# Transformer block with delta rule and dilated attention: the gate's modulation summed along with the second group's levels, sums of C11 made where they are read, T4 and the last turns on ScalarE

## The chip, the core and the metric

The kernel runs on one core of one Trainium2 chip. It has a matrix engine (TensorE, PE in the profile), a vector engine (VectorE, DVE), a scalar engine (ScalarE, ACT), GpSimd (POOL) and an engine that here only issues transfers (SyncE, SP). Each engine executes its own instructions strictly in the order in which the program lists them, and waits where an operand isn't there yet. The metric is the device time of one execution in microseconds. Three runs of the kernel before took 1418.77, 1416.32 and 1415.34 us; the median is 1416.32.

## The reference, cut to what matters

One block of a network over 1024 rows of 1024 columns, all in 32-bit floats:

```python
mod = silu(c) @ w_ada + b_ada                       # 6 parts of 1024: sh1, sc1, g1, sh2, sc2, g2
h = rmsnorm(x, norm_attn_g) * (1 + sc1) + sh1
q_a, k_a, v_a, q_d, k_d, v_d, z_d, b_d, a_d = split(h @ w_in)
y_attn = dilated_attention(q_a, k_a, v_a, rel_bias)   # 8 heads of 64
y_delta = gated_deltanet(q_d, ..., z_d)               # 8 heads of 64, 16 chunks of 64 rows
x = x + g1 * (concat(y_attn, y_delta) @ w_out)        # g1 is the gate of the change
h = rmsnorm(x, norm_ffn_g) * (1 + sc2) + sh2
x = x + g2 * ((silu(h @ w_gate) * (h @ w_up)) @ w_down)
return rmsnorm(x, final_norm_g)
```

`g1` is a row of 1024 numbers: the product of silu(c) with 1024 columns of `w_ada`, plus `b_ada`. The kernel uses it to scale the columns of `w_out`.

## The kernel before, in words

Every large product is made of three matmuls per 128x128x512 step: each operand is split into a high part (a rounded copy, `wh`, `hh`, `T3h`) and a low part (what the rounding left, `wl`, `hl`, `T3l`), and high x high, high x low and low x high are added up in one bank of the accumulator.

The program runs in these stages; times are in the span of the profiled execution. First comes the head with the norm and the first projections. Then the delta rule for heads 0 to 3 (`delta(0)`) and heads 4 to 7 (`delta(1)`). Each group has an inversion on DVE (31 pairs of small products into `tt`), a trip of the inverse through memory that reorders it (`tn_d`, then `tn`), a **level stage** that builds the larger blocks of the inverse for four heads (`head`: `lv` by PE, `cs` by DVE, `lb` by PE, `lw` by PE, `tc` by DVE, `lx` by PE), and a scan over eight double chunks (`delta_scan`). For the second group the inversion ends at 366 us, the level stage lies between 373 and 407 us, and the scan follows to about 449 us. While those small steps run, the remaining projections (`g_a`, `g_va`) fill PE between them; a table of numbers (`FILL`, `LEVELS`, `TURNS`) says how much of it goes where.

The **attention stage** (from about 455 us) runs over 32 units (a pair of heads and a block of 128 rows): `S` scores by PE, maximum by DVE into `sc`, exponential on ACT or POOL, turns `tr`, `et`, values. Projections go on between them until the eighth unit (`free`); after that the first half of the output product `wo` fills. In the same units the rest of the modulation is summed. A slab of `w_ada` (128 rows by 512 columns, 256 KB) is loaded by SP into one of two slots (`mod_in`, tile `wm`), DVE multiplies it by 128 values of silu(c) and adds it to a running sum (`mod_add`, line 1334 for the first of eight slabs, line 1336 for the others), and after eight slabs PE sums over the 128 partitions with a matmul of ones (`mod_out`, `mods`, line 1346). Slabs 0 to 15 are the gate `g1` (two halves of 512 columns; DVE adds each sum to a broadcast of the bias in `g1r`, line 1347), slabs 16 to 47 are later parts, 48 to 63 come in the last stage. `mod_until(n)` does slabs up to n: eight at the start, then one more with each unit until unit 8, then the others spread over the rest. `out_slab` loads a slab of `w_out`, multiplies it by `g1r` on POOL and splits it.

Then the first product of the last network starts (from about 700 us, `wg`, `wu`), while the rows of x are normed and turned (`out_turn`, half of the turns by DVE and half by ACT). It uses a recursive scheme with seven products per 2x2 blocks, whose operands are `H11`, `H21`, `T1`, `T2`, `T3`, `T4`, `H22`, each split by `h2_split` (high part by ACT, low part by DVE; for T4 both by DVE). `up_first` makes `C11`: one product into bank a, copied by ACT (`p1`), another into bank b, added by DVE. `up_rest` adds to bank a the product with T2, copies the bank (`u2`, line 1664), adds the T3 product to the same bank, and later the T4 product. So the T3 matmuls cannot start before the `u2` copy by ACT has read the bank, and the T4 matmuls not before the addition by DVE (line 1620, `wg_u`) has read it again. From about 814 us to the end PE works without a gap.

Of the kernel before, what the change touches and what calls it, by code (L numbers as in the profile page):

```python
# [10 lines left out]
F32 = mybir.dt.float32  # L11
# [7 lines left out]
P = 128  # L19
# [69 lines left out]
def build(tc, I, out):  # L89
# [890 lines left out]
    def delta_scan(g, st):  # L980
# [94 lines left out]
            nc.scalar.dma_start(_.yd[g][:, :, tk].rearrange("q p t -> p q t"), yt)  # L1075

        kept, outs = {}, {}
        for n in range(8 + 3):
            if n < 8:
                state(n)  # L1080
            if 1 <= n <= 8:
                outs[n - 1] = readout(n - 1, *kept.pop(n - 1))
            if n >= 3:
                flip(n - 3, outs.pop(n - 3))
# [21 lines left out]
    def va_end(c):  # L1106
        f = va_evac(c)

        def g(tb, ps):
            f(tb, ps)  # L1110
            if c == 0:
                nc.sync.dma_start(Rb_d[tb], R_d[tb : tb + 1, :].to_broadcast([P, 1152]))
        return g

    done = set()
    def others():
# [223 lines left out]
    def mod_out(i):  # L1340
        t0 = 16 + 4 * i
        acc = states[:, HALF * (i % 2) : HALF * (i % 2) + HALF]
        ps = tbank(f"mods{i}")
        if i < 2:
            cs = slice(HALF * i, HALF * i + HALF)
            nc.tensor.matmul(ps, ones, acc, start=True, stop=True)
            nc.vector.tensor_tensor(out=g1r[:, cs], in0=ps, in1=g1r[:, cs], op=ALU.add)
            return
        v = acc.rearrange("p (t j m) -> p j t m", j=4, m=32)
        for j in range(4):  # L1350
            nc.tensor.matmul(
                ps[32 * j : 32 * j + 32, 0:P], ones[:, 0:32], v[:, j], start=True, stop=True, skip_group_check=True
            )
        t = (pa if i < 6 else po2).tile([P, 256], F32, name=f"mt{i}", tag="mt", bufs=1)
        by_columns(ps, mod[:, t0 : t0 + 4], 4, bada[:, t0 : t0 + 4], shape=t)
        if i == 5:
            nc.vector.scalar_tensor_tensor(
                out=G2, in0=mod[:, 32:40], scalar=1.0, in1=gff, op0=ALU.add, op1=ALU.mult
            )
# [7 lines left out]
    def out_slab(k, s):  # L1367

        n = slabs_made[0]
        slabs_made[0] += 1  # L1370
        p, h, b = (pe, "e", 4) if n >= 12 else (wp, "w", 5) if n % 7 < 5 else (pr, "v", 2)
        raw = wp.tile([P, slot], F32, name=f"wr_wo{k}_{s}", tag="wr", bufs=3)
        hi = p.tile([P, slot], F32R, name=f"wh_wo{k}_{s}", tag=f"{h}h", bufs=b)
        lo = p.tile([P, slot], F32R, name=f"wl_wo{k}_{s}", tag=f"{h}l", bufs=b)
        with urgent():
            nc.sync.dma_start(raw, I["wo"][k * P : (k + 1) * P, columns(s)])
            nc.gpsimd.tensor_tensor(out=raw, in0=raw, in1=g1r[:, columns(s)], op=ALU.mult)
            nc.scalar.copy(hi, raw)
            nc.gpsimd.tensor_tensor(out=lo, in0=raw, in1=hi.bitcast(F32), op=ALU.subtract)
        return hi, lo  # L1380
# [34 lines left out]
    weight = [2.0 if qb < 4 else 1.0 for _hp, qb in units]  # L1415
    xs, ets = {}, {}
    loaded[0] = att_load(0)
    nc.sync.dma_start(g1r, I["bada1"].to_broadcast([P, D]))
    summed = [0]

    def mod_until(n):
        while summed[0] < n:
# [5 lines left out]
                turns_out.append(summed[0] // 8 - 1)  # L1428

    turns_out = []  # L1430
    for n in range(2):
        mod_in(n)
    ahead(LEAD)
    mod_until(8)
    for i in range(len(units) + AV):
        while turns_out:
            mod_out(turns_out.pop(0))
        mod_until(9 + i if i < free else 16 + -(-32 * (i - free + 1) // (len(units) + AV - free)))
        if i == free:
            run(fill[0])  # L1440
            share[0] = 0.0
            sh_.close()
            spv.close()
            pr, spr = pool("pr", side="right")
            py, sy = pool("py", side="right")
            pyd, syd = pool("pyd", side="right")
            for k in range(KT):
                p_ = py if k < 4 else pyd
                yh[k] = p_.tile([P, T], F32R, name=f"yh{k}", tag=f"yh{k}")
                yl[k] = p_.tile([P, T], F32R, name=f"yl{k}", tag=f"yl{k}")  # L1450
            for k in range(4, 8):
                y_load(k, _.yd[k // 2 - 2][k % 2])
            fill[0] = out_delta()
            spent[0] = 0.0
        if i < free:
            share[0] = (W_IN - spent[0]) * weight[i] / sum(weight[i:free]) / 2
        elif free < i < len(units):
            share[0] = (W_OUT - spent[0]) * weight[i] / sum(weight[i:]) / 2
        if i < len(units):
            hp, qb = units[i]  # L1460
            if hp not in loaded:
                loaded[hp] = att_load(hp)
            if qb >= 2 and hp < 3 and hp + 1 in done and hp + 1 not in loaded:
                loaded[hp + 1] = att_load(hp + 1)
            xs[i] = [att_score(hp, qb, e) for e in range(2)]
        if AT <= i < len(units) + AT:
            hp, qb = units[i - AT]
            ets[i - AT] = [att_turn(hp, qb, e, xs[i - AT][e]) for e in range(2)]
            del xs[i - AT]
        if i >= AV:  # L1470
            hp, qb = units[i - AV]
            att_value(hp, qb, ets.pop(i - AV))
        if i == free + 12:
            for k in range(EARLY):
                y_load(k, _.ya[k])
# [28 lines left out]
    def out_turn(tb, hs):  # L1504

        hf, ts_ = tb // 4, slice(tb % 4 * P, tb % 4 * P + P)
        for q in range(2):
# [4 lines left out]
            with urgent():  # L1512
                for j in range(4):
                    d = 4 * q + j
                    if j % 2:
                        nc.vector.tensor_scalar(
                            out=x2[d, hf][:, ts_], in0=ps[:, j * P : (j + 1) * P],
                            scalar1=G2[:, d : d + 1], scalar2=mod[:, 24 + d : 25 + d], op0=ALU.mult, op1=ALU.add,
                        )
                    else:  # L1520
                        nc.scalar.activation(
                            x2[d, hf][:, ts_], ps[:, j * P : (j + 1) * P], AF.Identity,
                            bias=mod[:, 24 + d : 25 + d], scale=G2[:, d : d + 1],
                        )
# [99 lines left out]
    def up_first(f, w, raws):  # L1624
# [4 lines left out]
        with urgent():  # L1629
            nc.scalar.copy(p1, a)  # L1630
        up_mm(b, raws[1], f"{w}{f}_12", "H21")
        with urgent():
            add(p1, b, p1)
        return a, p1
# [53 lines left out]

    def up_end(f, first):
        ag, g11, rg = first["wg"] if first else gate_first(f, "wg")  # L1690
        silu(g11, g11)
        if first:
            rg = again0 if f == 0 else raws_first(f, "wg")
# [3 lines left out]
        silu(g22, g22)  # L1697
        silu(g21, bank)
        au, c11, ru = first["wu"] if first else gate_first(f, "wu")

        a11, a12, a21, a22 = (po2.tile([P, HALF], F32, name=f"a{i}_{f}", tag=f"a{i}", bufs=1) for i in (11, 12, 21, 22))
        nc.vector.tensor_tensor(out=a11, in0=g11, in1=c11, op=ALU.mult)
# [63 lines left out]
        h2_split("H22", k, x2[4 + k, 1], nc.vector)  # L1766
    for k in range(4):
        sub(x2[4 + k, 0], x2[4 + k, 0], t2[k])
        h2_split("T4", k, x2[4 + k, 0], nc.vector, nc.vector.tensor_copy)
    sx.close()  # L1770
    po2, so2 = pool("po2")

# [234 lines left out]
```

## Time and profile before

| what | us |
|---|---|
| median of three runs | 1416.32 |
| the profiled execution, device time | 1419.05 |
| its span in the trace | 1417.3 |
| PE busy | 1341.3 (95%) |
| DVE busy | 926.0 (65%) |
| ACT busy | 658.3 (46%) |
| POOL busy | 286.9 (20%) |

The mean clock that was granted to PE is 0.986 of full speed. A row of the timeline gives the start in the span, the duration, the engine, the line of the program, the operation, the tiles written and read, their shapes, and in brackets the idle time of the engine just before it with what ended it. A row of the windows gives for a stretch of time the busy time of each engine with the number of instructions, the granted clock of PE, the share of the transfer engines that was in use, and the rate in GB/s.

### The profile page before, as it was taken

What the parts mean: (1) busy time and instruction counts of PE and PEld (TensorE: products, weight loads), DVE (VectorE), ACT (ScalarE), POOL (GpSimd) and SP (SyncE); (2) the same over time, 40 slices, a digit from 0 to 9 for tenths busy, and PEclk for the clock granted to TensorE, in tenths of its full rate; (3) what the DMA queues carried; (4) which work ended last, traced back from release to release, by engine and by line L of the source; (5) the groups of instructions that cost most, each with busy time, mean ns of one, the idle gap of its engine ahead of it and who ended that gap; (6) DMA issues with size and microseconds to landing.
All of it is one profiled execution on the core that took longest, in us unless ns stands there. A gap on an engine that the chain in (4) does not pass through costs nothing.

```text
span 1417.3 us, 23510 instructions
## 1 busy us (share of the span) xinstructions
PE 1341.3 (95%) x8504; PEld 1103.1 (78%) x8504; DVE 926.0 (65%) x1761; ACT 658.3 (46%) x1302; POOL 286.9 (20%) x260
## 2 busy tenths in 40 slices
PE   7998999899998878998999799999999999999997
PEld 4776977889798766676788688888888888888886
DVE  3687875667455246767637987757575776474487
ACT  3497444383323435555659433333333333444446
POOL 2335432435214344564500000000000000000000
PEclk9999999999999989999999899999999999999999
DMA  8764343443414956667343374546363656766667
GB/s 303 232 165 133 102 154 120 137 140 90 126 32 120 246 164 199 195 187 228 127 177 111 121 223 159 175 139 195 106 217 118 194 193 195 262 214 201 196 219 244
DMA packets 161886, 243.00 MB, mean 171 GB/s; under 512 B 32647, under 2 KB 67768, under 8 KB 161769
## 3 DMA queue, kind: packets, MB, share of 16 engines
q1 hardware_dynamic: 147048, 229.96, 51.8%
q10 hardware_dynamic: 14720, 11.54, 2.4%
q8 instruction: 67, 1.10, 0.3%
q14 instruction: 51, 0.41, 0.1%
HBM read 178.68 MB, written 67.48 MB: 174 GB/s over the span
## 4 chain that ended last, share of the span: by engine, by line
PE 67%; DVE 13%; DMA 8%; ACT 4%; issue 4%; POOL 3%; SPq 0%; ACTq 0%; DVEq 0%; POOLq 0%
PE wua L1611 8%; PE wga L1611 8%; PE X L1820 7%; PE wo L1387 5%; PE wuc L1611 4%; PE Z L1820 4%; PE wgc L1611 4%; DMA wm<-in_wada 3%; PE g_a L597 3%; PE g_va L620 3%; PE Y L1820 2%; PE wub L1611 2%; PE wgb L1611 2%; PE g_vd L597 2%; PE vd L505 1%
## 5 line engine op out<-in xcount | busy, mean ns | idle before, releaser
L1601 DVE TENSOR_TENSOR wl_db<-wr_db,wh_db 128x512 fp32r<-128x512 f32 x77 | 53.2, 691 | 76.2 <-ACT wh_db L1600 75.8
L1600 ACT CAST wh_db<-wr_db 128x512 fp32r<-128x512 f32 x77 | 47.9, 622 | 98.8 <-PE X L1820 41.3
L1273 ACT ACTIVATE X<-X,sc 128x128 f32<-128x128 f32 (+7 forms) x64 | 49.7, 777 | 75.3 <-DVE sc L1268 72.5
L1275 POOL TENSOR_SCALAR X<-X,sc 128x128 f32<-128x128 f32 (+7 forms) x64 | 50.2, 786 | 98.2 <-DVE sc L1274 88.3
L1336 DVE SCALAR_TENSOR_TENSOR states<-wm,cc,states 128x512 f32<-128x512 f32 x56 | 46.9, 837 | 35.0 <-DMA wm<-in_wada 34.7
L1820 PE MATMUL X<-wl_db,wh_da 128*128 128x512 f32 x176 | 68.7, 391 | 0.5 <-DVE wl_db L1601 0.5
L1820 PE MATMUL X<-wh_db,wl_da 128*128 128x512 f32 x176 | 68.6, 390 | 0.0
L1820 PE MATMUL X<-wh_db,wh_da 128*128 128x512 f32 x176 | 68.4, 390 | 0.0
L1387 PE MATMUL wo<-wh_wo,yl 128*128 128x512 f32 x128 | 51.0, 398 | 3.7 <-DVE yl L1411 3.7
L1387 PE MATMUL wo<-wh_wo,yh 128*128 128x512 f32 x128 | 54.0, 422 | 0.5 <-ACT yh L1410 0.5
L1601 DVE TENSOR_TENSOR wl_da<-wr_da,wh_da 128x512 fp32r<-128x512 f32 x77 | 52.7, 686 | 1.2 <-ACT wh_da L1600 1.2
L597 PE MATMUL g_a<-hh,wh_a 128*128 128x512 f32 x128 | 51.9, 406 | 0.0
L1287 PE MATMUL tr<-ident,X 128*128 128x128 f32 x288 | 44.7, 283 | 7.6 <-ACT et L1292 3.1
L597 PE MATMUL g_a<-hl,wh_a 128*128 128x512 f32 x128 | 51.7, 404 | 0.0
L1268 DVE CUSTOM_DVE_ANT_0 X<-S,ng 128x512 f32<-128x512 f32 (+3 forms) x64 | 37.4, 585 | 21.2 <-PE S L1265 16.0
L1387 PE MATMUL wo<-wl_wo,yh 128*128 128x512 f32 x128 | 51.2, 400 | 0.0
L597 PE MATMUL g_a<-hh,wl_a 128*128 128x512 f32 x128 | 51.0, 399 | 0.0
L1600 ACT CAST wh_da<-wr_da 128x512 fp32r<-128x512 f32 x77 | 47.3, 616 | 5.8 <-PE wua L1611 5.8
L1600 ACT CAST wh_wg_s<-wg_s 128x512 fp32r<-128x512 f32 x33 | 20.5, 622 | 59.7 <-PE wuc L1611 22.6
L1287 PEld LDWEIGHTS tr<-ident,X 128*128 128x128 f32 x288 | 33.6, 144 | 18.0 <-POOL X L1275 5.8
L1600 ACT CAST wh_wg<-wr_wg 128x512 fp32r<-128x512 f32 x33 | 20.5, 622 | 49.9 <-PE wua L1611 18.9
L1600 ACT CAST wh_wu_s<-wu_s 128x512 fp32r<-128x512 f32 x33 | 20.4, 620 | 49.6 <-PE wga L1611 16.5
(524 smaller groups left out, 4362.7 us busy)
## 6 DMA issues: line engine op xcount, KB each, us to landing
wr_da<-ao_d SPq DMA_DIRECT2D x77, 256.0 KB, 3.2
wm<-in_wada SPq DMA_DIRECT2D x64, 256.0 KB, 3.4
wr_wg<-in_wg SPq DMA_DIRECT2D x48, 256.0 KB, 3.1
wr_wu<-in_wu SPq DMA_DIRECT2D x48, 256.0 KB, 2.7
ao_d<-a SPq DMA_DIRECT2D x44, 256.0 KB, 2.8
wr_wd<-in_wdn SPq DMA_DIRECT2D x44, 256.0 KB, 3.1
wr_db<-wt_d SPq DMA_DIRECT2D x44, 256.0 KB, 2.7
ao_d<-as SPq DMA_DIRECT2D x33, 256.0 KB, 2.8
```

Source lines behind the costliest of these rows:

```text
L597: last[0] = nc.tensor.matmul(ps, a[:, w0], b[k0 + k4][:, cs], start=(i == 0), stop=(i == n - 1))
L620: last[0] = nc.tensor.matmul(ps[:, :n], a[k][:, ts_], b[:, w0], start=(i == 0), stop=(i == 23))
L1268: nc.vector.tensor_tensor_reduce(out=X[:, c0:c1], in0=ps[:, 0 : c1 - c0], in1=ng[:, u + c0 : u + c1], scale=1.0, scalar=(3e38 if m is None ...
L1273: nc.scalar.activation(X[:, 0:nk], X[:, 0:nk], AF.Exp, scale=-1.0, bias=m, accum_out=sc[:, 2:3])
L1275: nc.gpsimd.tensor_scalar(out=X[:, 0:nk], in0=X[:, 0:nk], scalar1=sc[:, 3:4], scalar2=0.0, op0=ALU.mult, op1=ALU.add)
L1287: nc.tensor.transpose(ps[:, (kb - c0) * P : (kb - c0 + 1) * P], X[:, kb * P : kb * P + P], ident)
L1336: nc.vector.scalar_tensor_tensor(out=acc, in0=w, scalar=cc[:, k : k + 1], in1=acc, op0=ALU.mult, op1=ALU.add)
L1387: last[0] = nc.tensor.matmul(ps, a[k0 + k][:, ts_], b, start=(k == 0 and n == 0), stop=(k == 3 and n == 2))
L1600: nc.scalar.copy(hi, src)
L1601: (eng or nc.vector).tensor_tensor(out=lo, in0=src, in1=hi.bitcast(F32), op=ALU.subtract)
L1611: last[0] = nc.tensor.matmul(ps, a[:, w0], b, start=(first and k == 0 and n_ == 0), stop=(k == 3 and n_ == 2), skip_group_check=True,)
L1820: nc.tensor.matmul(bank[b], a[:, ts_], w, start=(first and f == 0 and n_ == 0), stop=(f == NF - 1 and n_ == 2), skip_group_check=True,)
```

## The change

Three things change.

First, the sixteen slabs of the gate `g1` leave the attention stage. Their loads (`gate_in`) and sums (`gate_add`) are written in `delta_scan` of the second group, two per double chunk, with slots from the tag `tm` (two, shared with the small products of the inversion). The sum runs in `g1r` itself, which POOL sets to zero early in the program and whose first row is loaded with the bias. Two matmuls of ones (`gate_out`) at the units 1 and 2 of the attention sum over the partitions, and ACT copies the result back into `g1r`. In the attention the sums then begin with slab 16 and go on at one per unit up to slab 47; the eight slabs at its start and the broadcast of the bias are gone.

Second, in the first two blocks of the last network `up_first` no longer adds the second bank into `C11` by DVE out of the accumulator: ACT copies bank b too (`p2`), and DVE adds the two copies in `up_end`, just before they are read. The high parts of T4 are rounded by ACT instead of DVE, and the last block of rows is turned by ACT alone.

Third, slab 11 of `w_out` takes its slots from another pool (`pr` instead of `wp`).

```diff
--- before.py
+++ after.py
@@ -1075,9 +1075,16 @@
             nc.scalar.dma_start(_.yd[g][:, :, tk].rearrange("q p t -> p q t"), yt)
 
         kept, outs = {}, {}
+        if g == 1:
+            for n in range(2):
+                gate_in(n)
         for n in range(8 + 3):
             if n < 8:
                 state(n)
+                if g == 1:
+                    for i in (2 * n, 2 * n + 1):
+                        gate_add(i)
+                        gate_in(i + 2)
             if 1 <= n <= 8:
                 outs[n - 1] = readout(n - 1, *kept.pop(n - 1))
             if n >= 3:
@@ -1111,6 +1118,31 @@
             if c == 0:
                 nc.sync.dma_start(Rb_d[tb], R_d[tb : tb + 1, :].to_broadcast([P, 1152]))
         return g
+
+
+    gate_w = {}
+    nc.gpsimd.memset(g1r, 0.0)
+    nc.sync.dma_start(g1r[0:1, :], I["bada1"])
+
+    def gate_in(n):
+        if n < 16:
+            i, k = n // KT, n % KT
+            gate_w[n] = pd.tile([P, HALF], F32, name=f"wm_{i}_{k}", tag="tm", bufs=2)
+            nc.sync.dma_start(gate_w[n], I["wada"][k * P : (k + 1) * P, 2 * D + HALF * i : 2 * D + HALF * i + HALF])
+
+    def gate_add(n):
+        i, k = n // KT, n % KT
+        acc = g1r[:, HALF * i : HALF * i + HALF]
+        nc.vector.scalar_tensor_tensor(
+            out=acc, in0=gate_w.pop(n), scalar=cc[:, k : k + 1], in1=acc, op0=ALU.mult, op1=ALU.add
+        )
+
+    def gate_out(i):
+
+        ps = tbank(f"gate{i}")
+        acc = g1r[:, HALF * i : HALF * i + HALF]
+        nc.tensor.matmul(ps, ones, acc, start=True, stop=True)
+        nc.scalar.copy(acc, ps)
 
     done = set()
     def others():
@@ -1341,11 +1373,6 @@
         t0 = 16 + 4 * i
         acc = states[:, HALF * (i % 2) : HALF * (i % 2) + HALF]
         ps = tbank(f"mods{i}")
-        if i < 2:
-            cs = slice(HALF * i, HALF * i + HALF)
-            nc.tensor.matmul(ps, ones, acc, start=True, stop=True)
-            nc.vector.tensor_tensor(out=g1r[:, cs], in0=ps, in1=g1r[:, cs], op=ALU.add)
-            return
         v = acc.rearrange("p (t j m) -> p j t m", j=4, m=32)
         for j in range(4):
             nc.tensor.matmul(
@@ -1368,7 +1395,7 @@
 
         n = slabs_made[0]
         slabs_made[0] += 1
-        p, h, b = (pe, "e", 4) if n >= 12 else (wp, "w", 5) if n % 7 < 5 else (pr, "v", 2)
+        p, h, b = (pe, "e", 4) if n >= 12 else (pr, "v", 2) if n in (5, 6, 11) else (wp, "w", 5)
         raw = wp.tile([P, slot], F32, name=f"wr_wo{k}_{s}", tag="wr", bufs=3)
         hi = p.tile([P, slot], F32R, name=f"wh_wo{k}_{s}", tag=f"{h}h", bufs=b)
         lo = p.tile([P, slot], F32R, name=f"wl_wo{k}_{s}", tag=f"{h}l", bufs=b)
@@ -1415,8 +1442,7 @@
     weight = [2.0 if qb < 4 else 1.0 for _hp, qb in units]
     xs, ets = {}, {}
     loaded[0] = att_load(0)
-    nc.sync.dma_start(g1r, I["bada1"].to_broadcast([P, D]))
-    summed = [0]
+    summed = [16]
 
     def mod_until(n):
         while summed[0] < n:
@@ -1428,14 +1454,15 @@
                 turns_out.append(summed[0] // 8 - 1)
 
     turns_out = []
-    for n in range(2):
+    for n in range(16, 18):
         mod_in(n)
     ahead(LEAD)
-    mod_until(8)
     for i in range(len(units) + AV):
+        if i in (1, 2):
+            gate_out(i - 1)
         while turns_out:
             mod_out(turns_out.pop(0))
-        mod_until(9 + i if i < free else 16 + -(-32 * (i - free + 1) // (len(units) + AV - free)))
+        mod_until(16 + min(i, 32))
         if i == free:
             run(fill[0])
             share[0] = 0.0
@@ -1512,7 +1539,7 @@
             with urgent():
                 for j in range(4):
                     d = 4 * q + j
-                    if j % 2:
+                    if j % 2 and tb < TB - 1:
                         nc.vector.tensor_scalar(
                             out=x2[d, hf][:, ts_], in0=ps[:, j * P : (j + 1) * P],
                             scalar1=G2[:, d : d + 1], scalar2=mod[:, 24 + d : 25 + d], op0=ALU.mult, op1=ALU.add,
@@ -1629,6 +1656,12 @@
         with urgent():
             nc.scalar.copy(p1, a)
         up_mm(b, raws[1], f"{w}{f}_12", "H21")
+        if f < AHEADF:
+
+            p2 = po.tile([P, HALF], F32, name=f"p2_{w}{f}", tag="p2", bufs=4)
+            with urgent():
+                nc.scalar.copy(p2, b)
+            return a, (p1, p2)
         with urgent():
             add(p1, b, p1)
         return a, p1
@@ -1688,6 +1721,9 @@
 
     def up_end(f, first):
         ag, g11, rg = first["wg"] if first else gate_first(f, "wg")
+        if first:
+            add(g11[0], *g11)
+            g11 = g11[0]
         silu(g11, g11)
         if first:
             rg = again0 if f == 0 else raws_first(f, "wg")
@@ -1697,6 +1733,9 @@
         silu(g22, g22)
         silu(g21, bank)
         au, c11, ru = first["wu"] if first else gate_first(f, "wu")
+        if first:
+            add(c11[0], *c11)
+            c11 = c11[0]
 
         a11, a12, a21, a22 = (po2.tile([P, HALF], F32, name=f"a{i}_{f}", tag=f"a{i}", bufs=1) for i in (11, 12, 21, 22))
         nc.vector.tensor_tensor(out=a11, in0=g11, in1=c11, op=ALU.mult)
@@ -1766,7 +1805,7 @@
         h2_split("H22", k, x2[4 + k, 1], nc.vector)
     for k in range(4):
         sub(x2[4 + k, 0], x2[4 + k, 0], t2[k])
-        h2_split("T4", k, x2[4 + k, 0], nc.vector, nc.vector.tensor_copy)
+        h2_split("T4", k, x2[4 + k, 0], nc.vector)
     sx.close()
     po2, so2 = pool("po2")
 
```

The program is ordered by a scheduler, so the instructions do not stand where the text has them. The place of the level stage, on DVE: `tt` is the last step of the inversion, `U`, `cs`, `tc` are steps of the levels, `g1r<-wm` is a sum of the gate. Before:

```order
L900 TENSOR_TENSOR tt_3816<-tt_3816,tm_30_3909 128x31
L936 STREAM_TRANSPOSE U_0_4337<-tn_3912 32x8x32 x4
L942 TENSOR_TENSOR cs_0_4339<-lv_0_4340,nbp_1350 32x256 x2
L962 TENSOR_TENSOR tc_0_4338<-lw_0_4410,nbp_1350 64x512
L942 TENSOR_TENSOR cs_1_4427<-lv_1_4428,nbp_1350 32x256
```

and in the changed kernel (three sums stand ahead of `U` in the order, of which the third is shown):

```order
L1136 SCALAR_TENSOR_TENSOR g1r<-wm_2_4779,cc,g1r 128x512
L936 STREAM_TRANSPOSE U_0_4339<-tn_3914 32x8x32 x4
L1136 SCALAR_TENSOR_TENSOR g1r<-wm_3_4782,cc,g1r 128x512
L1136 SCALAR_TENSOR_TENSOR g1r<-wm_4_4807,cc,g1r 128x512
L1136 SCALAR_TENSOR_TENSOR g1r<-wm_5_4810,cc,g1r 128x512
L1136 SCALAR_TENSOR_TENSOR g1r<-wm_6_4852,cc,g1r 128x512
L1136 SCALAR_TENSOR_TENSOR g1r<-wm_7_4855,cc,g1r 128x512
L1136 SCALAR_TENSOR_TENSOR g1r<-wm_0_4899,cc,g1r 128x512
L942 TENSOR_TENSOR cs_0_4341<-lv_0_4342,nbp_1352 32x256 x2
L1136 SCALAR_TENSOR_TENSOR g1r<-wm_1_4902,cc,g1r 128x512
L1136 SCALAR_TENSOR_TENSOR g1r<-wm_2_4962,cc,g1r 128x512
L962 TENSOR_TENSOR tc_0_4340<-lw_0_4412,nbp_1352 64x512
```

Six sums stand between the first head's `U` and its `cs`, and two between `cs` and `tc`; five more follow before the `tc` of the second, third and fourth head, so that all sixteen stand in the level stage and none in the scan. The queue of SP at the same place, in the changed kernel (`tn_d` and `tn` are the trip of the inverse through memory, `wr_a` slabs of the projections):

```order
L1131 DMA wm_0_4759<-in_wada 128x512
L907 DMA tn_d<-tt_3818 128x1024
L1131 DMA wm_1_4761<-in_wada 128x512
L1131 DMA wm_2_4779<-in_wada 128x512
L237 DMA wr_a_1_0_5305<-in_wd 128x512
L908 DMA tn_3914<-tn_d 128x32x32
L237 DMA wr_a_1_1_5311<-in_wd 128x512
L1131 DMA wm_3_4782<-in_wada 128x512
L1131 DMA wm_4_4807<-in_wada 128x512
L1131 DMA wm_5_4810<-in_wada 128x512
```

Before, `tn_d`, one `wr_a` and `tn` followed each other there; now three slabs of the gate are issued around them, and the others one by one as their slots come free.

The start of the last network, on ACT. Before, the copies of bank a (`wg_u<-wga`) and bank c followed the casts of T3:

```order
L1537 CAST T3h_8539<-x_2_1_7962 128x512
L1537 CAST T3h_8541<-x_3_1_7963 128x512
L1664 COPY wg_u_8853<-wga_8555 128x512
L1666 COPY wg_u_8854<-wgc_8774 128x512
```

and in the changed kernel:

```order
L1564 CAST T3h_8542<-x_3_1_7964 128x512
L1564 CAST T4h_8544<-x_4_0_7969 128x512
L1564 CAST T4h_8546<-x_5_0_7970 128x512
L1564 CAST T4h_8548<-x_6_0_7971 128x512
L1564 CAST T4h_8550<-x_7_0_7972 128x512
L1720 ACTIVATE p_wg_8676<-p_wg_8676 128x512
L1697 COPY wg_u_8859<-wga_8556 128x512
L1699 COPY wg_u_8860<-wgc_8779 128x512
```

The four casts of T4 and a silu of the second block now stand between the casts of T3 and the copy of bank a. The silu reads a sum of `C11` that DVE makes at its row 981, after the subtraction that the last T4 cast reads.

## The prediction

> **What bounds the kernel now.** I read the totals first, then the windows of 25 us, then the waits of PE in the three stretches that the change touches, and last the timeline rows there.
>
> ```profile
> span 1417.3 us, 23510 instructions
> PE 1341.3 (95%) x8504; PEld 1103.1 (78%) x8504; DVE 926.0 (65%) x1761; ACT 658.3 (46%) x1302; POOL 286.9 (20%) x260
> ```
>
> PE is busy for 1341.3 of 1417.3 us, so 76 us are all that waits can give back, plus what a lowered clock costs. Where they lie is told by the windows (columns: busy time of PE, of its weight loads, of DVE, ACT and POOL, each with the number of instructions; granted clock of PE; share of the transfer engines; GB/s):
>
> ```profile
> 375.00:400.00 25.00, 23.63 (x446) 21.23 (x447) 8.62 (x19) 9.63 (x26) 5.69 (x6) 1.00 0.19 60
> 450.00:475.00 25.00, 25.00 (x108) 20.57 (x108) 2.88 (x4) 9.09 (x16) 7.56 (x5) 0.96 0.81 229
> 475.00:500.00 25.00, 16.59 (x75) 13.19 (x74) 8.98 (x22) 7.99 (x21) 7.66 (x8) 0.93 0.90 231
> 500.00:525.00 25.00, 21.69 (x94) 16.42 (x94) 11.16 (x21) 7.94 (x20) 13.69 (x11) 0.91 0.54 159
> 525.00:550.00 25.00, 22.83 (x129) 17.88 (x129) 13.68 (x41) 11.84 (x25) 8.81 (x9) 0.89 0.53 157
> 550.00:575.00 25.00, 19.83 (x131) 13.14 (x129) 20.50 (x29) 13.93 (x27) 18.23 (x13) 0.93 0.68 213
> 795.00:820.00 25.00, 18.64 (x62) 14.63 (x63) 23.81 (x42) 7.80 (x14) 0.00 (x0) 0.80 0.51 166
> 820.00:845.00 25.00, 25.00 (x112) 20.72 (x111) 22.89 (x37) 9.16 (x17) 0.00 (x0) 1.00 0.72 222
> ```
>
> PE is full at 450 to 475 and from 820 on. The start of attention loses 8.41 us in one window (25 less 16.59) with the transfers at 0.90, the start of the last network 6.36 us with DVE at 23.81 of 25. The levels (375 to 400) look harmless: PE at 23.63, DVE at 8.62. The longest waits of PE, for 455 to 575, 372 to 408 and 770 to 830 us (the line waiting, what it waits for, total, times, longest):
>
> ```profile
> PE mods L1346 <- DVE states L1336: 7.3, 1, 7.3
> PE S L1264 <- DVE sc L1268: 4.8, 4, 3.0
> PE tr L1287 <- DVE g1r L1347: 0.6, 1, 0.6
> PE g_va L620 <- ACT sp_a L1102: 1.7, 1, 1.7
> PE wga L1611 <- DVE wg_u L1620: 3.7, 1, 3.7
> PE wga L1611 <- ACT wg_u L1664: 3.6, 1, 3.6
> ```
>
> **Attention, where the gate's sums leave.** The gate's first half must be complete before its matmul of ones, which stands in PE's order ahead of everything else.
>
> ```profile
> 497.88 0.75 DVE L1336 SCALAR_TENSOR_TENSOR states<-wm,cc,states 128x512 f32<-128x512 f32 x1 [4.09 <-DMA wm<-in_wada]
> 500.11 2.08 PE L1346 MATMUL mods<-states,onesr 128*128 128x512 f32 x2 [7.26 <-DVE states L1336]
> 502.05 0.78 PE L597 MATMUL g_a<-hl,wh_a 128*128 128x512 f32 x1
> 523.12 0.75 DVE L1336 SCALAR_TENSOR_TENSOR states<-wm,cc,states 128x512 f32<-128x512 f32 x1 [1.66 <-DMA wm<-in_wada]
> 534.30 0.75 DVE L1336 SCALAR_TENSOR_TENSOR states<-wm,cc,states 128x512 f32<-128x512 f32 x1 [2.29 <-DMA wm<-in_wada]
> ```
>
> The matmul waits 7.26 us, the eighth sum having waited for a slab. The changed kernel has no such sum here: its two matmuls find `g1r` summed since the levels. That is 7.3 us, and the 0.6 us behind line 1347. The 4.8 us of `S` waiting for `sc` come where DVE stands at a sum whose slab isn't there (1.66 and 2.29 us in the rows), with the next maximum queued behind it. Sixteen slabs are now summed in the units that took 24, so each has more time to land, but they still stand in clumps of two; I take 3.3 of the 4.8. Third, the clock: 0.91 and 0.89 in the two windows from 500 to 550 are 5.0 us of full clock (9% and 11% of 25), and the matmul at 502.05 took 0.78 us. Part of that falls into time in which PE stands anyway, so I charge 3.0. Against it I set 2.0 us for what ends last next: the loads of `yl` and of `raw`, which this change leaves; their bound is 0 to 5.2, all that PE misses in the window from 550. Sum: 7.3 + 0.6 + 3.3 + 3.0 - 2.0 = 12.2 us gained; from 3 (7.3 + 0.6, less a new wait of 5.2) to 17.7 (7.3 + 0.6 + 4.8 + 5.0, and no new wait).
>
> **The levels, where they go.** Timeline rows of DVE and SP there:
>
> ```profile
> 365.93 0.19 DVE L900 TENSOR_TENSOR tt<-tt,tm 128x31 f32<-128x31 f32 x1
> 366.15 0.33 SPq L907 DMA_DIRECT2D tn_d<-tt  x1
> 369.00 0.38 SPq L908 DMA_DIRECT2D tn<-tn_d  x1
> 373.46 1.78 DVE L936 STREAM_TRANSPOSE U<-tn 32x256 f32<-32x256 f32 x4 [7.33 <-DMA tn<-tn_d]
> 381.15 0.86 DVE L942 TENSOR_TENSOR cs<-lv,nbp 32x256 f32<-32x256 f32 x2 [5.91 <-PE lv L931]
> 384.77 0.69 DVE L962 TENSOR_TENSOR tc<-lw,nbp 64x512 f32<-64x512 f32 x1 [2.76 <-PE lw L960]
> 391.71 0.69 DVE L962 TENSOR_TENSOR tc<-lw,nbp 64x512 f32<-64x512 f32 x1 [2.86 <-PE lw L960]
> L1336 DVE SCALAR_TENSOR_TENSOR states<-wm,cc,states x56: 726/751/2464, 480.2 to 853.7; 128x512 f32<-128x512 f32 x56
> DMA to landing us min/median/max: 2.6/3.6/7.8
> ```
>
> DVE is idle for 7.33, 5.91, 2.76 and 2.86 us around the first two heads, and the sixteen sums need 16 x 0.75 = 12.0, so the work as such would fit. The order does not let it. Two slots hold the slabs, and a slab is issued only when the sum two before it has been made; the pace is one landing L, plus 0.75 for the sum and 0.1 to issue, for every two sums. The last row gives L: 2.6, 3.6, 7.8 us (least, median, most of 80). Three sums fit before `tn` lands. But SP now issues slabs around `tn_d` and `tn`; I delay each of the two by 1.0 us (median less least landing), so the four transposes of `U` begin at 375.5 instead of 373.46 and end at 377.2. The fourth sum, whose slab has landed by then, ends at 378.0. Sums five and six, seven and eight follow at L + 0.85 a pair, the ninth 0.75 behind; only then comes `cs`: 378.0 + 2(L + 0.85) + 0.75, with L = 3.6 at 387.65 instead of 381.15, 6.5 us late. The `tc` behind it stands after two further sums, the second of which ends L + 0.85 = 4.45 us after the ninth; in the trace `tc` begins 3.62 us after `cs`, so this adds 0.8. The later heads are 6.94 us apart (384.77 to 391.71), which covers a pair. The loss is 7.3 us.
>
> Does it reach the end? PE works in order, and behind `lv` it has little of the filling projections before `lb` needs `cs`: about nine `g_va` matmuls, some 1 us. Against this 1 us of cover stands the slower clock that a stall of 5 to 6 us leaves behind (the row at 502.05), so I let the two cancel. The Trainium skill, "TensorE: Matmul & The Clock Gate", section "Why this matters for your kernels", puts PE back to half its clock after an idle gap of over about 3 us, as the trace has it after 7.26 us; by that page's 3.4 us until full speed the tail is an estimate of 1.7 us, 0.7 more than the cover, and the time would be 1411.2. With L = 2.6 and no delay of `tn` the loss is 2.5; with 2.6 and the delay 4.5; with 7.8 it is 14.9 at `cs`, 5.0 at the first `tc` and 1.7 each at the second and third, 23.3. I take 7.3, by the median, since the transfers there are used at 0.19 but the slabs come on top.
>
> The Trainium skill, page "DMA: Bandwidth & Descriptors", section "Anatomy of one DMA", puts a transfer at about 2.0 us fixed plus its bytes at 436 GB/s, an estimate of 2.6 us for 256 KB; this agrees with the least landing in the row above, not with its median. By the page alone the loss would be 4.5 us and the time 1407.7. The same page ("Rules for kernel authors") advises to issue early and wait late; two slots whose refill waits for DVE do the opposite.
>
> **The start of the last network.**
>
> ```profile
> 776.63 0.40 DVE L1516 TENSOR_SCALAR x<-x2t,G,mod 128x128 f32<-128x128 f32 x1
> 796.99 0.58 ACT L1664 COPY wg_u<-wga 128x512 f32<-128x512 f32 x1
> 797.63 0.79 PE L1611 MATMUL wga<-T3h,wh_wg_s 128*128 128x512 f32 x1 [3.55 <-ACT wg_u L1664]
> 798.22 0.63 PE L1611 MATMUL wga<-T3l,wh_wg_s 128*128 128x512 f32 x1
> 799.21 1.28 DVE L1617 TENSOR_TENSOR x<-x,t 128x512 f32<-128x512 f32 x2
> 800.42 0.75 DVE L1537 CAST T4h<-x 128x512 fp32r<-128x512 f32 x2
> 809.09 0.68 DVE L1620 TENSOR_TENSOR wg_u<-wga,wg_u 128x512 f32<-128x512 f32 x1
> ```
>
> DVE sheds four T4 casts of 0.38 and four turns of 0.40, together 3.1 us; the four sums of `C11` stay at some 0.6 each and only move. But the `u2` copy of bank a now stands behind the T4 casts and a silu that wait for DVE's last subtractions. Following DVE's order in steps of 0.60 (two subtractions from 799.21 to 800.42), the sum that the silu reads ends at about 801.3, the silu at 801.95 and the copy at 802.5: T3 begins 4.9 us later than 797.63. In exchange the second wait goes: T3's twelve matmuls and H22's twelve (first 0.43 apart, as from 798.22 in the trace, then 0.22 to 0.23 as at full clock, 112 in the 25 us from 820) run to about 810.7, while the addition into `wg_u` is done by 808. T4 then ends at about 813.4, against 814.3 before (809.83 and twelve more). Gain 0.9, between -4.9 (if the second wait of 3.7 stays behind the later T3) and 3. The third edit, another slot for slab 11, lies in 725 to 775 us where no wait of PE is among those listed; I cost it at nothing, and at 1 us if the first loads of `wg` land late.
>
> **The sum.** 12.2 - 7.3 + 0.9 = 5.8 us off. The profiled execution took 1419.05 (span 1417.3, the rest around it), 2.7 above the median; 1419.05 - 5.8 = 1413.2 on its basis, and 1416.3 - 5.8 = 1410.5 for the median of runs. A difference under 0.3% (4.25 us) counts as none.
>
> **Rivals.**
>
> *The sums vanish in DVE's idle time.* For it: 18.9 us of DVE idle in the four rows of the level stage against 12.0 of work; if slabs land in 2.6 and PE's `lv` comes late anyway, little is lost. Against it: six sums stand ahead of one `cs`. With 1 us lost: 1416.3 - 12.2 - 0.9 + 1.0 = 1404.2.
>
> *The attention wait is only replaced.* For it: transfers at 0.90, and PE at 19.83 of 25 in the window from 550, whose waits the change leaves. Against it: PE is full until 475 and the gate's slabs were among the transfers behind that 0.90. If 4 of the 12.2 come: 1416.3 - 4 + 7.3 - 0.9 = 1418.7.
>
> *Slower: slabs land in the levels as slowly as at the worst.* One mechanism, at the six sums before `cs`: each pair costs a whole landing. It decides from L = 5.3, where the loss equals 13.1 (4.7 gives 10.6 by the same working, 7.8 gives 23.3); at 7.8 the time is 1416.3 - 13.1 + 23.3 = 1426.5. For it: the most in the row. Against it: a share of 0.19 there.
>
> *T3's late copy isn't paid back.* If T4 waits for `wg_u` as it did, 4.9 are lost instead of 0.9 won: 1416.3.
>
> **Chances and range.** Forecast 0.52, with its own range 1405 to 1415: 0.40 faster by more than 4.25, 0.12 the same. Sums hidden 0.15, all faster. Attention replaced 0.16: 0.11 the same, 0.05 slower. Slow slabs 0.08: 0.07 slower, 0.01 the same. T3 not paid back 0.09: 0.02, 0.06, 0.01. Together faster 0.57, same 0.30, slower 0.13. The range reaches from 1402 (below the hidden case) to 1418.7 (the replaced wait) and leaves out the slow slabs and the edges.
>
> **What would show it.** In the profile after: `cs` of the first head starting 5 to 8 us later after `tt` than the 15.2 of now, with DVE idle before the sums for their slabs; no `mods` wait near 500, and the window there above 21 of PE; T3 waiting some 8 us for the copy by ACT and T4 nothing. I am wrong if the first `cs` is no later than now, if the wait of 7.3 returns under another name, or if T4 waits too.

## The result, and the profile after

The changed kernel takes 1434.78 us (median of 4 runs, 1432.12 to 1437.78) against 1416.09 before: 1.0129 times as long, with a 95% interval of 1.0105 to 1.0153. It is 18.7 us slower; 5.8 us faster had been forecast. (Of experiment e7 below the profiled execution, 1427.64 us, lies far over the others of that kernel; the comparisons leave it out.)

The head of the page of the changed kernel:

```profile
span 1436.1 us, 23542 instructions
PE 1360.5 (95%) x8504; PEld 1122.9 (78%) x8504; DVE 918.4 (64%) x1751; ACT 664.9 (46%) x1316; POOL 287.2 (20%) x261
```

PE executes the same 8504 matmuls and is busy 19.2 us longer (1360.5 less 1341.3), while its idle time is 75.6 us against 76.0. So on balance nothing of the loss is waiting: new waits stand against old ones that went, and the same work ran slower. First, two more windows of the kernel before:

```profile
400.00:425.00 25.00, 24.30 (x271) 22.82 (x266) 13.73 (x46) 6.88 (x21) 4.87 (x6) 1.00 0.13 38
425.00:450.00 25.00, 21.22 (x168) 20.18 (x168) 17.35 (x49) 9.08 (x25) 13.57 (x14) 0.97 0.30 89
```

and those of the changed kernel:

```profile
375.00:400.00 25.00, 19.10 (x216) 17.46 (x219) 14.43 (x23) 7.56 (x20) 3.78 (x4) 0.64 0.56 165
400.00:425.00 25.00, 25.00 (x321) 22.42 (x315) 8.83 (x17) 4.07 (x10) 1.91 (x2) 0.50 0.12 39
425.00:450.00 25.00, 25.00 (x165) 24.24 (x161) 9.63 (x35) 5.49 (x16) 3.86 (x5) 0.66 0.07 22
450.00:475.00 25.00, 22.19 (x185) 21.20 (x183) 17.78 (x55) 9.52 (x27) 12.24 (x14) 1.00 0.26 75
475.00:500.00 25.00, 23.66 (x100) 19.58 (x101) 3.77 (x3) 7.36 (x14) 8.60 (x6) 0.93 0.79 222
500.00:525.00 25.00, 22.11 (x97) 17.13 (x96) 7.59 (x22) 12.52 (x29) 12.53 (x11) 1.00 0.88 235
525.00:550.00 25.00, 21.88 (x114) 17.65 (x113) 13.02 (x28) 7.39 (x20) 12.44 (x12) 1.00 0.70 197
```

The third number from the right is the one to see. The granted clock is 0.64, 0.50 and 0.66 from 375 to 450 us, where the kernel before had 1.00, 1.00 and 0.97, and from 400 us on PE reads as fully busy all the while. The same stretch in steps of 10 us, first before, then changed:

```profile
380.00:390.00 10.00, 10.00 (x230) 8.89 (x229) 4.13 (x9) 3.18 (x9) 1.47 (x3) 1.00 0.28 87
390.00:400.00 10.00, 10.00 (x194) 8.91 (x193) 4.25 (x9) 3.24 (x9) 1.91 (x2) 1.00 0.05 16
```

```profile
380.00:390.00 10.00, 5.72 (x108) 5.27 (x108) 5.73 (x7) 1.03 (x4) 1.68 (x2) 0.84 0.72 216
390.00:400.00 10.00, 10.00 (x96) 8.80 (x98) 5.55 (x11) 2.22 (x6) 1.25 (x2) 0.50 0.31 78
...
430.00:440.00 10.00, 10.00 (x55) 9.66 (x55) 2.17 (x9) 1.85 (x5) 0.61 (x1) 0.50 0.04 13
440.00:450.00 10.00, 10.00 (x81) 9.92 (x80) 6.76 (x25) 2.55 (x8) 3.25 (x4) 0.90 0.14 39
```

Ten microseconds of the levels hold 96 matmuls at half clock where they held 194. Ahead of it stand the first two of these waits of PE (`lb` writes into the bank of `lv`, so the second is the wait of `lb` for `cs`); the third is at the start of the last network:

```profile
PE g_va L620 <- ACT sp_a L1109: 5.4, 1, 5.4
PE lv L946 <- DVE cs L942: 4.3, 1, 4.3
PE wga L1638 <- ACT wg_u L1697: 8.5, 1, 8.5
```

The wait for `sp_a` was 1.7 us before. The rows of DVE that make the second one:

```profile
374.91 1.78 DVE L936 STREAM_TRANSPOSE U<-tn 32x256 f32<-32x256 f32 x4 [2.58 <-DMA tn<-tn_d]
376.75 1.60 DVE L1136 SCALAR_TENSOR_TENSOR g1r<-wm,cc,g1r 128x512 f32<-128x512 f32 x2
380.35 2.67 DVE L1136 SCALAR_TENSOR_TENSOR g1r<-wm,cc,g1r 128x512 f32<-128x512 f32 x2 [1.99 <-DMA wm<-in_wada]
385.57 0.75 DVE L1136 SCALAR_TENSOR_TENSOR g1r<-wm,cc,g1r 128x512 f32<-128x512 f32 x1 [2.56 <-DMA wm<-in_wada]
386.63 0.75 DVE L1136 SCALAR_TENSOR_TENSOR g1r<-wm,cc,g1r 128x512 f32<-128x512 f32 x1 [0.31 <-DMA wm<-in_wada]
387.41 0.86 DVE L942 TENSOR_TENSOR cs<-lv,nbp 32x256 f32<-32x256 f32 x2
```

Six sums stand between `U` and `cs`, as in the order. They go in pairs: the first finds its slabs there, the second and the third wait for theirs. `cs` starts at 387.41 (forecast 387.65).

Where the time went, by the starts of the last `tt`, the first `cs`, the last turn of the scan (`yt`), the first and last `wo`, and the first T2 matmul of `wu` in the profiled executions (us between them; e4 and e6 are experiments below):

| from, to | before | changed | difference | e4 | e6 |
|---|---|---|---|---|---|
| start, end of inversion | 365.9 | 363.8 | -2.2 | 362.9 | 362.0 |
| inversion, first `cs` | 15.2 | 23.7 | +8.4 | 18.1 | 23.2 |
| first `cs`, end of scan | 67.3 | 88.9 | +21.6 | 73.8 | 71.5 |
| end of scan, first `wo` | 114.6 | 104.0 | -10.6 | 98.2 | 105.6 |
| first `wo`, last `wo` | 201.4 | 203.6 | +2.2 | 199.0 | 199.3 |
| last `wo`, T2 of `wu` | 49.8 | 48.9 | -0.9 | 48.8 | 48.9 |
| T2 of `wu`, end of span | 603.0 | 603.2 | +0.2 | 603.4 | 603.0 |

### The profile page after: what moved, and what is told of

It reads as the page before. It is cut to its first block, busy times and chain, and to the rows that moved or that the text cites. A ratio compares the mean times of both kernels' runs of the same rounds, so it can differ in the third digit from the quotient of the medians.

```text
span 1436.1 us, 23542 instructions
## 1 busy us (share of the span) xinstructions
PE 1360.5 (95%) x8504; PEld 1122.9 (78%) x8504; DVE 918.4 (64%) x1751; ACT 664.9 (46%) x1316; POOL 287.2 (20%) x261
## 4 chain that ended last, share of the span: by engine, by line
PE 67%; DVE 14%; DMA 9%; POOL 4%; ACT 3%; issue 3%; SPq 0%; ACTq 0%; DVEq 0%; POOLq 0%
PE wga L1638 8%; PE wua L1638 8%; PE X L1859 7%; PE wo L1414 5%; PE wuc L1638 4%; PE wgc L1638 4%; PE Z L1859 4%; DMA wm<-in_wada 2%; PE Y L1859 2%; DVE tt L900 2%; PE g_va L620 2%; DVE tm L896 2%; PE g_a L597 2%; PE wgb L1638 2%; PE wub L1638 2%
## 5 line engine op out<-in xcount | busy, mean ns | idle before, releaser
L620 PE MATMUL g_va<-wh_va,hh 128*128 128x256 f32 x128 | 44.4, 347 | 5.4 <-ACT sp_a L1109 5.4
L1368 DVE SCALAR_TENSOR_TENSOR states<-wm,cc,states 128x512 f32<-128x512 f32 x42 | 34.9, 831 | 21.6 <-DMA wm<-in_wada 21.6
L620 PE MATMUL g_va<-wl_va,hh 128*128 128x256 f32 x128 | 41.8, 327 | 2.3 <-POOL wl_va L239 2.3
```

Of the source, the lines that this page charges most:

```text
L620: last[0] = nc.tensor.matmul(ps[:, :n], a[k][:, ts_], b[:, w0], start=(i == 0), stop=(i == 23))
L1368: nc.vector.scalar_tensor_tensor(out=acc, in0=w, scalar=cc[:, k : k + 1], in1=acc, op0=ALU.mult, op1=ALU.add)
```

## Experiments

After the result the theory was: the gap before the first head's `lb` lets the granted clock fall to 0.50, and the levels and the scan, in which several hundred matmuls with outputs from 32x32 to 128x128 alternate with larger ones of 128x256, hold a full clock but do not raise a halved one for a long time ("half clock held"). (From 388 to 441 us the changed kernel's trace has 92 of the larger ones, busy for 40.9 of these 53 us; they are not few.) The first rival: the sums and their 4 MB of slabs delay the stage themselves. Each run has its own runs of the kernel before on the same chip beside it; ratios are against those.

**e1, the gate's sums back in the attention.** Edit, against the changed kernel:

```diff
-    summed = [16]
+    nc.sync.dma_start(g1r, I["bada1"].to_broadcast([P, D]))
+    summed = [0]
...
-        if i in (1, 2):
-            gate_out(i - 1)
```

> The gate's sums go back to the attention stage; the other two edits stay (C11 sums where they are read, T4 and last turns by ScalarE, slab 11's pool). All theories that blame the level stage: the level stage is as before with the clock at 1.00, T3 waits about 8 us for ScalarE's copy and T4 not at all, time 1414 to 1417. Rival 'the other edits cost it': 1430 to 1437.

Measured: 1415.87 us, ratio 1.0002 (0.9984 to 1.0019). The whole loss belongs to the moved sums. The other two edits together are worth nothing that can be measured, though T3 waits its 8.5 us here too. In this profile PE also waits 4.5 us for `sp_a`, and the clock is 0.50 from 380 to 385 us behind it; it is back before the first `cs` at 388.3 and stays at 1.00 through the levels. So a longer wait for `sp_a` comes without the moved sums too, and did no lasting harm here.

**e2, clock kept.** Edit, with matmuls that add nothing to the result:

```diff
-            with turn(f"lb{g}_{hl_}"):
+            with turn(f"lb{g}_{hl_}"), ExitStack() as behind:
+                if g == 1 and hl_ == 0:
+                    junk = ybank("junk")
+                    for i in range(18):
+                        spin = nc.tensor.matmul(junk, hh[i % 4][:, 0:P], hl[i % 4][:, 0:HALF], start=True, stop=True)
+                    behind.enter_context(tc.issue_after(spin.ins))
```

> The changed kernel plus 18 matmuls of 128x512 whose result nobody reads, on PE just before the first head's lb, where PE stood idle for 4.28 us. Theory 'half clock held' (the idle gap drops the granted clock to 0.50 and the small matmuls of levels and scan never raise it): clock 1.00 from 383 us to the end of the scan, last tc of the levels near 410 instead of 428.6, time about 1434.8 - 19 = 1416 (1412 to 1419). Rival 'sums and slab traffic in the way': the levels stay as late as in the changed kernel, 1433 to 1439.

Measured: 1428.37, ratio 1.0094 (1.0068 to 1.0119). Neither number. The windows of this run tell why:

```profile
385.00:390.00 5.00, 4.26 (x80) 3.51 (x79) 3.02 (x5) 1.09 (x3) 0.65 (x1) 1.00 0.57 161
390.00:395.00 5.00, 2.75 (x56) 2.36 (x54) 3.32 (x6) 0.37 (x1) 0.30 (x1) 1.00 0.60 170
395.00:400.00 5.00, 4.51 (x69) 3.95 (x68) 2.97 (x6) 2.37 (x6) 0.30 (x1) 0.56 0.27 76
400.00:405.00 5.00, 5.00 (x56) 4.59 (x54) 3.34 (x8) 0.37 (x1) 0.96 (x1) 0.50 0.08 26
```

The clock got past the gap ahead of `lb`. At 393.97 us ends the next one, a wait of `lx` of 2.25 us that the following sums make, and within 2 us behind it the clock falls. e6 fills that too.

**e3, the stall alone, in the kernel before.** Edit:

```diff
...
+                    nc.vector.memset(junk, 0.0)
+                    for i in range(16):
+                        spin = nc.vector.scalar_tensor_tensor(
+                            out=junk, in0=junk, scalar=cc[:, 0:1], in1=junk, op0=ALU.mult, op1=ALU.add
+                        )
+                slow.enter_context(tc.issue_after(spin.ins))
...
```

> The kernel before with nothing of the change, plus 16 idle vector operations (12 us of DVE, no transfers) between the first head's U and its cs, so that cs starts near 387.5 and PE waits some 5 us. Theory 'half clock held': clock 0.50 from there through the levels and the first steps of the scan, loss 6 for the wait and about 20 for the clock, time 1436 to 1446. Rival 'sums and slab traffic in the way': only the wait is lost, 1421 to 1424.

Measured: 1432.67 (1425.03 to 1440.78), ratio 1.0122 (1.0072 to 1.0172). No slab, no sum, no other edit, and the runs lose 9 to 25 us, at the median more than the rival's and less than the theory's numbers. Windows of its profiled execution, which took 1429.79 us:

```profile
390.00:395.00 5.00, 1.30 (x40) 1.10 (x41) 4.79 (x9) 0.00 (x0) 0.00 (x0) 0.92 0.01 2
395.00:400.00 5.00, 5.00 (x55) 4.59 (x49) 1.37 (x3) 1.15 (x4) 0.95 (x1) 0.50 0.00 0
...
410.00:415.00 5.00, 5.00 (x110) 4.32 (x110) 0.92 (x3) 1.93 (x5) 0.00 (x0) 0.87 0.01 3
415.00:420.00 5.00, 5.00 (x98) 4.52 (x96) 3.29 (x7) 0.85 (x2) 0.95 (x1) 1.00 0.07 26
```

The clock falls at the gap, but comes back after some 17 us, within the levels, where in the changed kernel it took some 55. In this execution `cs` comes 26.1 us after the inversion (15.2 before), and the way from there to the end of the scan takes 74.2 us (67.3 before). So 10.9 us are the stall itself and 6.9 lie behind it (the way to the first `wo` is then 8.2 us shorter). e3 shows that a gap without slabs and sums lets the clock fall, and that how long it stays down varies; it doesn't show the 20 us for the clock. Whether its longer runs held the half clock longer is not on record.

**e4, sums spread.** Edit, in place of two per scan step in the text (the first two loads are also issued behind the load of `tn` instead of around it):

```diff
...
+        places = ['cs0', 'cs0', 'cs1', 'cs1', 'cs2', 'cs2', 'cs3', 'cs3', 'tc3', 's0', 's1', 's2', 's3', 's4', 's5', 's6']
+        def sums(i):
+            with tc.issue_after(st["dv"][places[i]].ins):
+                gate_add(i)
+            gate_in(i + 2)
...
```

> The changed kernel with the same sixteen sums and slabs, but issued so that no cs or tc waits for them: the first two slabs behind the load of tn, two sums behind each head's cs, one behind the last tc, one behind each of seven scan steps. Theory 'half clock held': no idle gap, clock 1.00 through levels and scan, levels end within 3 us of before (tc last at 404 to 409), and the 10 us of the attention and 1 us of the last network stay: 1403 to 1409. Rival 'sums and slab traffic in the way': the same work in the same stage costs again, 1424 to 1436.

Measured: 1407.21, ratio 0.9948 (0.9929 to 0.9967): faster than before. Sixteen sums and sixteen slabs are still in levels and scan.

```profile
380.00:390.00 10.00, 10.00 (x230) 8.88 (x229) 6.82 (x13) 3.18 (x9) 1.25 (x2) 1.00 0.34 107
390.00:400.00 10.00, 10.00 (x195) 8.91 (x193) 6.17 (x12) 3.14 (x9) 1.91 (x2) 1.00 0.40 122
```

The clock is 1.00, the matmuls per 10 us are those of before (230 and 195), with DVE busier and the slabs in flight. The rival falls: the work as such does not slow the levels. It costs 6.5 us from `cs` to the end of the scan (73.8 against 67.3), and the way to the first `wo` is 16.4 us shorter. Which of the two, the places of the sums or the later first loads, did more is not tested.

**e5, re-warm.** Edit, against the changed kernel: 20 matmuls behind `lb`, where e2 had 18 before it.

```diff
...
+            if g == 1 and hl_ == 0:
+                junk = ybank("junk")
+                with tc.issue_after(spun.ins):
+                    for i in range(20):
+                        last[0] = nc.tensor.matmul(junk, hh[i % 4][:, 0:P], hl[i % 4][:, 0:HALF], start=True, stop=True)
```

> The changed kernel plus 20 matmuls of 128x512, whose result nobody reads, on PE right behind the first head's lb, that is after the gap, where the clock stood at 0.50. Theory 'half clock held' (the levels' small matmuls keep a full clock but cannot raise a halved one; a run of large ones raises it): the burst takes 5 to 6 us, the clock is 1.00 behind it through levels and scan, last tc near 412 instead of 428.6, time 1434.8 + 6 - 20 = 1420 (1415 to 1425). Rival 'the stage runs at half clock whenever it is late': the clock falls back at once, 1438 to 1442.

Measured: 1420.94, ratio 1.0031 (1.0012 to 1.0049): added work makes the changed kernel 14 us faster.

```profile
385.00:390.00 5.00, 1.63 (x50) 1.47 (x51) 2.65 (x5) 0.48 (x2) 0.00 (x0) 0.74 0.53 163
390.00:395.00 5.00, 5.00 (x15) 3.90 (x14) 2.40 (x4) 0.61 (x2) 0.00 (x0) 0.58 0.39 112
395.00:400.00 5.00, 5.00 (x69) 4.37 (x68) 2.24 (x5) 0.37 (x1) 0.95 (x1) 1.00 0.34 104
400.00:405.00 5.00, 5.00 (x97) 4.49 (x95) 3.43 (x7) 2.38 (x6) 0.30 (x1) 1.00 0.32 84
```

The burst starts at 389.4 us and the clock is back at about 394.1; from there the levels keep it.

**e6, all gaps filled.** Edit: the loop of e2 also before the first head's `lx` and the second head's `lb`.

```diff
...
+                if g == 1 and hl_ < 2:
+                    spin_on(behind, (18, 6)[hl_])
...
+                if g == 1 and hl_ == 0:
+                    spin_on(behind, 12)
...
```

> As e2 (the changed kernel with 18 unread matmuls before the first lb), and also 12 before the first head's lx and 6 before the second head's lb, where e2 still left gaps of 2.25 us and after which its clock fell to 0.50 at 395 us. Theory 'half clock held': clock 1.00 through all of the levels and the scan, the scan's end 94 to 100 us after the last tt instead of 112.6 in the changed kernel, time 1414 to 1422. Rival 'sums and slab traffic in the way': no better than e2's 1428.

Measured: 1413.93, ratio 0.9983 (0.9965 to 1.0001).

```profile
390.00:400.00 10.00, 10.00 (x139) 8.37 (x133) 6.30 (x11) 2.50 (x7) 0.30 (x2) 1.00 0.43 121
400.00:410.00 10.00, 9.83 (x187) 8.72 (x188) 6.45 (x13) 2.41 (x6) 1.91 (x2) 1.00 0.09 29
```

With the clock at 1.00 from 380 to 430 us the way from `cs` to the end of the scan takes 71.5 us, with the badly ordered sums and 36 matmuls for nothing, against 88.9 without those matmuls. That is 17.4 us for the held half clock, in the stage where the clock differs. The medians differ by 1434.8 - 1413.9 = 20.9 us, more than the whole loss; of the profiled executions' 22.5, the 5 beyond those 17.4 lie elsewhere, 4.3 of them between the first and the last `wo`, where the edit changes nothing. So the clock's worth is some 17 to 21 us.

**e7, copies by GpSimd**, and **e8, the copy early**, both on e4:

```diff
-            nc.scalar.copy(t64[0:32, :, 0:32], tnh[0:32])
+            (nc.gpsimd.tensor_copy if g == 1 else nc.scalar.copy)(t64[0:32, :, 0:32], tnh[0:32])
...
```

> e4 (sums spread) with the eight copies of tn into the levels' operands by GpSimd instead of ScalarE, which in e4 held ScalarE until tn had landed, so that PE waited 4.4 us for sp_a at 376 us. If that wait is ScalarE's queue: it falls under 1.5 us and the slower clock behind it goes as well, 3 to 6 us less than e4's 1407.2, 1401 to 1404. If PE would have waited for something else by then: within 1.5 us of e4.

```diff
+    u0 = po.tile([P, HALF], F32, name="wg0_u2", tag="u0", bufs=1)
+    with urgent():
+        copied = nc.scalar.copy(u0, early[0]["wg"][0])
...
+        with tc.issue_after(copied.ins):
+            h2_split("T4", k, x2[4 + k, 0], nc.vector)
```

> e4 (sums spread) with the copy u2 of bank a ahead of the T4 casts in ScalarE's order (its tile in a pool of its own, one slot less for the second half's weights). If the 8.5 us for which T3 waits are ScalarE's order: T3 starts about 8 us earlier, H22 then waits some 3 us for the copy of bank c that still stands behind the casts, and T4 ends 4 to 5 us earlier: 1402 to 1404. If DVE's sums end last anyway: 1406 to 1408.

Measured: e7 1403.32, ratio 0.9909 (0.9883 to 0.9935); e8 1405.12, ratio 0.9926 (0.9898 to 0.9954). e7 lies in the better of its two ranges and e8 between its two, but their intervals overlap that of e4, so neither step is shown to gain by its time.

e7's trace is that of the execution named above. In it the wait for `sp_a` is gone, but PE waits 3.6 us for `wl_va` by GpSimd instead, so the gap has only changed its cause. Behind it ten matmuls of 128x256 run for 2.4 us at half clock, then the levels begin, and the clock stays at 0.50 until about 434 us. So in this execution a gap ahead of the levels was enough to hold the half clock through them.

In e8's profile T3 no longer waits and H22 waits 5.8 us for the copy of bank c instead; the way from the last `wo` to T2 of `wu` takes 45.8 us (48.8 in e4). But `wua` then waits 4.1 us for a sum by DVE (0.4 in e4), and the way from T2 to the end takes 609.0 us where e4 has 603.4. e8 also leaves one slot less for the weights of the second half; which of the two costs this is not tested.

**e9, together**: e8 with ScalarE's copies of `tn` behind its copy of `sp_a`.

```diff
+            with tc.issue_after(spilled[0].ins) if g == 1 else ExitStack():
+                nc.scalar.copy(t64[0:32, :, 0:32], tnh[0:32])
...
```

> e8 (sums spread, u2 copy early) with ScalarE's copies of tn into the levels' operands put behind its copy of the last projection (sp_a), so that PE does not wait for that copy ahead of the levels (4.4 us in e4, followed by about 4 us at half clock). If that gap is ScalarE's order: it falls to under 1 us, the clock stays 1.00 from 370 us on, and the time is 2 to 5 us under e8's 1405.1: 1400 to 1403. If something else (wl_va by GpSimd, the slabs) holds PE there: 1404 to 1406.

Measured: 1402.86, ratio 0.9922 (0.9896 to 0.9947), in the first of its two ranges. The wait for `sp_a` is gone from its profile and the clock is 1.00 throughout 365 to 400 us, yet the ratio is e8's. e8's own profile already had only 1.0 us of that wait, so this doesn't tell what the 4.4 us of e4 were worth. e9 beats both kernels, the one before by 0.8%.

## Why the prediction was wrong

- **Attention**, 12.2 us forecast: the way from the end of the scan to the first `wo` became 10.6 us shorter, and the `wo` stage 2.2 longer. The `mods` wait is gone and the clock in the two windows from 500 is 1.00. `S` still waits 3.6 us for `sc` (4.8 before; 1.5 had been left), and the new `gate` matmul waits 2.0 us for ACT. The mechanism is right, the size is open: e1 and e3 keep the sums in the attention and take 109.2 and 106.4 us for that way against 114.6 before, so part of the 10.6 comes without the change. Against e1 the way is 3.6 (e6) to 11.0 us (e4) shorter without the sums, with the scan ending at nearly the same time (455 to 457 us).
- **The late `cs`**, 6.5 us forecast: counted from the end of the inversion it is 8.4, just beyond the 5 to 8 named as the sign. `U` begins 11.1 us after the inversion (7.5 before), 3.6 later where 2.0 had been allowed for the delayed `tn`; the sums behind it add 4.8 (4.5 forecast). The start itself, 387.41 against 387.65, fits so well by luck, as the inversion ended 2.2 us sooner. The 16 slabs landed in 2.7 to 5.8 us, 3.0 at the median (L had been 3.6). Right in mechanism, 1.9 us too small.
- The prediction sets a slab against a fit from the Trainium skill, "DMA: Bandwidth & Descriptors", section "Anatomy of one DMA". That page gives the fit for transfers issued by GpSimd, and the slabs are issued by SP, so its agreement with the least landing of 2.6 us compares two different paths.
- **The clock behind it** is the step that failed. "Against this 1 us of cover stands the slower clock that a stall of 5 to 6 us leaves behind [...], so I let the two cancel": the slower clock did not last some 3 us as behind the stall at 500 us, but 55. PE's wait for `cs` was 4.3 us, and the way from `cs` to the end of the scan grew by 21.6; e6 takes 17.4 of these away with the same sums in the same order and the clock kept, so it is the clock and not the sums. I had read the length of the tail from a stall that large matmuls follow, and applied it to a stage in which small ones stand between them. The sum with that term measured: -10.6 + 2.2 + 8.4 + 21.6 - 0.9 = 20.7 us slower; with 2.2 us less up to the inversion and 0.2 at the end it is the 18.8 between the two spans, but for rounding. In the profiles that end of the inversion lies anywhere from 362 to 370 us, so no cause is sought for 2 us there.
- **The last network**, 0.9 us forecast: 0.9 in the profile, T3 waiting 8.51 us (8 forecast) and T4 not at all. e1 says that it can't be told from nothing in time.
- **Rivals.** "Slow slabs" had the sign, 1426.5 us, but not the mechanism: the slabs landed no slower than forecast. (Its limit is also off: by the prediction's own working the loss reaches 13.1 us at L = 5.5, not 5.3.) "The sums vanish in DVE's idle time" (1404.2) comes near what the order of e4 gives, 1407.2. "T3's copy not paid back" fell, as T4 doesn't wait. "Attention only replaced" is not settled: its gain of 4 us lies at the lower end of the comparison with e1.

## What to carry to other kernels

Before work is put into the idle time of a helper engine, find the instruction behind it that PE waits for, and look at which matmuls follow: a gap of 2 to 5 us ahead of a stage of mostly small matmuls can cost the half clock over the whole stage, which here came to some 17 to 21 us, and not only the gap. Read the granted clock of each stage beside its busy share, since a PE at half clock reads as fully busy. The same sums, ordered behind the instructions that PE waits for instead of ahead of them, and with their first loads behind that of `tn`, turned 1.3% slower into 0.5% faster.

## What the runs showed of the hardware

Large matmuls back to back raised the granted clock from 0.50 to 1.00 within about 4 to 5 us: 3.8 us behind the wait for `sp_a` in the changed kernel (376.6 to 380.4), and 4.7 in e5; 2.4 us of them were not enough in e7's trace. The Trainium skill ("TensorE: Matmul & The Clock Gate", section "What's actually happening") gives some 3.4 us of sustained work for it; the traces lie a little above. The mix of the levels, in which PE reads as busy with hardly a break, took about 17 us (e3), 41 us (e2) and 55 us (the changed kernel) to do the same; there the measurement differs from that rule, if the busy share of the profile is what it means. What in that mix the clock counts as idle is not shown. And the clock fell behind gaps of 2.25 us (e2) and 4.3 us (the changed kernel, ahead of `lb`), though the wait of 1.7 us for `sp_a` in the kernel before had left it at 1.00; the wait of 5.4 us for `sp_a` in the changed kernel didn't.
